# Seven block products in place of eight in the output and gate projections of a decoder layer

## The chip, the cores and the metric

One Trainium2 chip, one core. Times are device microseconds (us). The kernel before takes 2246.29 us, the median of three timed runs (2245.44 to 2246.73).

## The reference

One decoder layer with 1024 tokens and width 2048. Four token mixers (A to D) work on 512 channels each; the two matrices that the change touches, `w_out` and `w_pg`, come behind them.

```python
h = x @ w_in[i]                        # 15 blocks of 512 columns
...                                    # four mixers: y_a, y_b, y_c, y_d
y = jnp.concatenate([y_a * silu(g_a), y_b * silu(g_b),
                     y_c * silu(g_c), y_d * silu(g_d)], axis=-1) @ w_out[i]
x = _layer_norm(ALPHA * x + y, ln_g[i], ln_b[i])
x = x + (p[i] @ w_pe[i]) * jax.nn.sigmoid(x @ w_pg[i])
```

`w_out` and `w_pg` are 2048 x 2048, `w_pe` is 256 x 2048. All is float32.

## The kernel before

**Numbers.** A product of float32 matrices is made of three matmuls: each operand is split into a high part, rounded by a cast on ScalarE (ACT, L142), and a low part, the rest, by a subtraction on VectorE (DVE, L143). TensorE (PE) multiplies high by high, low by high and high by low into the same PSUM bank. A *split* below is this cast and subtraction together.

**First part, to about 1483 us.** The products with `w_in` (proj L188, proj_tok L213) run on PE, and the four mixers are written as Python generators in a queue: step() advances the mixer at its head after every few matmuls, so that its instructions stand between those of the projections. Each mixer ends by storing its 128 channels x 1024 tokens to DRAM as y_dram; the last store is L303, of y_dram3.

**Output projection, L680 to L714.** The mixed channels are loaded back (L636) and split once, into yh and yl. phase2 runs for each half of the tokens (h, 512 tokens) and each of four blocks of 512 columns (n). token_mm (L641, matmul at L650) goes through 16 blocks of 128 channels: for each it loads 128 x 512 of W (load_w, L145 to L152, a DMA of 256 KB), splits it, and does 12 matmuls: four token tiles of 128 by three, into four PSUM banks called tk. So one half and one column block are 192 matmuls, and one projection is 8 x 192 = 1536. DVE then adds the banks to z, which holds x (L690, scaled by ALPHA), and takes the statistics for the layer norm (L691). Weights come twice, once for each token half. The norm of a half (L703, L704 on DVE, with the rows lg and lbias) and the transposes for the next stage (L708) stand in the queue and run beside the next half's matmuls; the normed tokens are stored as xln_dram.

**Gate projection, L716 to L736.** phase3 has the same loops with `w_pg`. Behind each 192 matmuls stand 24 small ones with p and w_pe (L665), ACT's sigmoid, DVE's product and sum (L733, L734, with xr, a piece of xln_dram loaded back), and the store of the result.

**What sets the order.** A tile scheduler orders the instructions by the order in which they are written, and puts what is written under `high_priority(offset=4000)` as far ahead as its buffers allow. Each engine then runs its own instructions in that order; an instruction that waits holds up all behind it on its engine. All DMAs are issued by SyncE (SP), in SP's order. load_w is under high priority, with 3 raw buffers and 4 each of wh and wl. PSUM has two pools of four banks of 512 columns: pp and mx; successive blocks of 192 matmuls take them in turn, so the reads of one set of banks lie beside the matmuls of the other. The pool act has 16 tiles of 1 MB.

Of the kernel before, what the change touches and what calls it, by code (L numbers as in the profile page):

```python
# [41 lines left out]
def trunk_kernel(  # L42
# [44 lines left out]
    # the first loads are under way: load the activation tables, bring the tensor engine up  # L87
# [7 lines left out]
    # softmax over the depth axis, its running sum less the first layer's share  # L95
# [31 lines left out]
    # mixers are traced in steps, a step after every few products of the projections that  # L127
    # follow, so that what a step's products wait for is done when the tensor engine gets there
# [25 lines left out]
    KORD = list(range(4, NK)) + [0, 1, 2, 3]  # L154

    # ======== phase 1: projections and token mixers, channels on partitions ========
    with tc.tile_pool(name="work", bufs=1) as work:
# [41 lines left out]
        def proj_tok(blk, banks, evac_tok, before=lambda k: None):  # L199
            # tokens on partitions: one tile of 128 tokens by 512 channels in each bank  # L200
# [52 lines left out]
        def transpose_to(dst, src):  # L253
            # dst[:, c, :] is the transpose of src[:, c, :], in blocks of 128
# [11 lines left out]
        def rms(o):  # L266
            # o: [token, chunk, channel]; the root mean square is over the head's channels
# [68 lines left out]
        def mix_b(j, kt, lt, qt, gts):  # L336
# [55 lines left out]
            # decays to the chunk's end and from its start  # L392
# [13 lines left out]
            for b in range(2):  # L406
# [3 lines left out]
                # one bank: only its first product clears the marks of what was written  # L410
# [217 lines left out]
        # the mixed channels come back, split, into the slots that x leaves  # L628
        yh = [[act.tile([P, 4, H], F32R, tag="act", name=f"yh{g}{h}") for g in range(4)] for h in range(2)]
        yl = [[act.tile([P, 4, H], F32R, tag="act", name=f"yl{g}{h}") for g in range(4)] for h in range(2)]  # L630
        raws = {}
        free_tags = ("x1", "v1", "E", "W", "a1", "q1", "E", "W", "vt")
        for ki, k in enumerate(KORD):
            tag = free_tags[ki % len(free_tags)]
            raws[k] = wtE() if tag == "E" else wtW() if tag == "W" else wt(tag)
# [170 lines left out]
```

## Time and profile before

| | |
|---|---|
| median of three runs | 2246.29 us |
| span of the profiled execution | 2243.6 us (the profile gives no other time for it) |
| TensorE (PE) busy | 2236.3 us, 100% |
| VectorE (DVE) busy | 958.6 us, 43% |
| ScalarE (ACT) busy | 674.9 us, 30% |
| the output and gate stages | 1483 to 2243.6 us |

Busy shares are of the span. The chain of waits follows the work that ended last back to the start, and its shares say whose time the span is. A grouped line gives the busy time of all its instructions and the mean of one in ns, then the idle time just before them with what ended it.

### The profile page before, as it was taken

To read this page: it belongs to the slowest core of one execution; us is meant where nothing else is said; L and a number is where in the kernel's file an instruction comes from. 1 tells how busy PE (TensorE), PEld (TensorE's weight loads), DVE (VectorE), ACT (ScalarE), POOL (GpSimd) and SP (SyncE) were. 2 spreads that over 40 slices of the span, in tenths; PEclk is the share of its full clock that TensorE was granted. 3 is DMA by queue.
4 is the path that set the end of the run, shared out by engine and by line. 5 is a ranking of instruction groups with operands and counts; after the bars stand their busy time and mean duration, and the time that the engine had idled before them with its cause. 6 is when DMAs were issued, how large, how long until landed. Compare 5 with 4: busy or idle time off the path is not lost.

```text
span 2243.6 us, 26997 instructions
## 1 busy us (share of the span) xinstructions
PE 2236.3 (100%) x10670; PEld 1867.0 (83%) x10670; DVE 958.6 (43%) x1670; ACT 674.9 (30%) x1201; POOL 43.7 (2%) x33
## 2 busy tenths in 40 slices
PE   9999999999999999999999999999999999999999
PEld 8888888888888888888888888888888888888887
DVE  5155565542555755431212212253365358333333
ACT  4144444432432433311211111142223224222222
POOL 0000000000000000000000000000000000000000
PEclk9999999999999999999999999999999999999999
DMA  6311111133111112421211111164345326444443
GB/s 232 96 42 48 46 53 45 56 108 103 43 57 38 57 57 80 142 70 57 94 57 57 50 59 57 48 225 134 96 135 179 113 95 237 133 136 132 136 148 106
DMA packets 112845, 216.33 MB, mean 96 GB/s; under 512 B 11856, under 2 KB 20304, under 8 KB 111440
## 3 DMA queue, kind: packets, MB, share of 16 engines
q1 hardware_dynamic: 112720, 214.62, 30.2%
q8 instruction: 83, 1.36, 0.2%
q14 instruction: 42, 0.34, 0.0%
HBM read 185.22 MB, written 29.36 MB: 96 GB/s over the span
## 4 chain that ended last, share of the span: by engine, by line
PE 99%; DVE 1%; ACT 0%; issue 0%; ACTq 0%; DVEq 0%
PE pp L188 46%; PE tk L650 31%; PE tok L213 12%; PE tk L665 2%; PE gram L362 2%; PE pv L539 1%; PE sc L494 1%; PE att L529 1%; PE sc L495 1%; PE xt L708 1%; PE hgo L414 0%; PE sv L601 0%; PE yt L282 0%; PE gram L347 0%; PE upd L409 0%; PE hgo L431 0%
## 5 line engine op out<-in xcount | busy, mean ns | idle before, releaser
L188 PE MATMUL pp<-xh,wh 128*128 128x512 f32 x1536 | 481.8, 394 | 0.0
L188 PE MATMUL pp<-xl,wh 128*128 128x512 f32 x1536 | 474.5, 390 | 0.0
L188 PE MATMUL pp<-xh,wl 128*128 128x512 f32 x1536 | 473.3, 389 | 0.0
L143 DVE TENSOR_TENSOR wl_t<-raw_t,wh_t 128x512 fp32r<-128x512 f32 x336 | 231.1, 690 | 493.0 <-ACT wh_t L142 452.9
L142 ACT CAST wh_t<-raw_t 128x512 fp32r<-128x512 f32 x336 | 209.2, 623 | 626.4 <-PE tk L650 463.1
L143 DVE TENSOR_TENSOR wl<-raw,wh 128x512 fp32r<-128x512 f32 x192 | 132.5, 690 | 498.0 <-ACT wh L142 483.9
L188 PEld LDWEIGHTS pp<-xl,wh 128*128 128x128 f32 x1536 | 288.4, 188 | 60.8
L188 PEld LDWEIGHTS pp<-xh,wl 128*128 128x128 f32 x1536 | 288.3, 188 | 60.3
L188 PEld LDWEIGHTS pp<-xh,wh 128*128 128x128 f32 x1536 | 281.8, 188 | 53.0
L142 ACT CAST wh<-raw 128x512 fp32r<-128x512 f32 x192 | 119.3, 621 | 637.7 <-PE pp L188 602.7
L650 PE MATMUL tk<-wh_t,yh 128*128 128x512 f32 x512 | 200.8, 392 | 0.0
L650 PE MATMUL tk<-wh_t,th 128*128 128x512 f32 x512 | 200.5, 392 | 0.0
L650 PE MATMUL tk<-wl_t,th 128*128 128x512 f32 x512 | 199.5, 390 | 0.0
L650 PE MATMUL tk<-wh_t,yl 128*128 128x512 f32 x512 | 199.4, 389 | 0.0
L650 PE MATMUL tk<-wl_t,yh 128*128 128x512 f32 x512 | 199.4, 390 | 0.0
L650 PE MATMUL tk<-wh_t,tl 128*128 128x512 f32 x512 | 199.3, 389 | 0.0
L213 PE MATMUL tok<-wh_t,xh 128*128 128x512 f32 x384 | 151.4, 394 | 0.0
L213 PE MATMUL tok<-wh_t,xl 128*128 128x512 f32 x384 | 149.9, 390 | 0.0
L213 PE MATMUL tok<-wl_t,xh 128*128 128x512 f32 x384 | 149.6, 390 | 0.0
L650 PEld LDWEIGHTS tk<-wh_t,yh 128*128 128x128 f32 x512 | 96.1, 188 | 20.2 <-DVE z L690 0.3
L650 PEld LDWEIGHTS tk<-wl_t,th 128*128 128x128 f32 x512 | 96.1, 188 | 20.3
L650 PEld LDWEIGHTS tk<-wl_t,yh 128*128 128x128 f32 x512 | 96.1, 188 | 20.1
(223 smaller groups left out, 2122.5 us busy)
## 6 DMA issues: line engine op xcount, KB each, us to landing
raw<-in_w_in_dram SPq DMA_DIRECT2D x192, 256.0 KB, 2.6
raw_t<-in_w_out_dram SPq DMA_DIRECT2D x128, 256.0 KB, 2.6
raw_t<-in_w_pg_dram SPq DMA_DIRECT2D x128, 256.0 KB, 2.7
raw_t<-in_w_tok_dram SPq DMA_DIRECT2D x80, 256.0 KB, 2.6
z<-in_x_dram SPq DMA_DIRECT2D x32, 256.0 KB, 4.5
xln_dram<-z SPq DMA_DIRECT2D x8, 1024.0 KB, 5.6
xr<-xln_dram SPq DMA_DIRECT2D x32, 256.0 KB, 3.8
out_dram<-sg SPq DMA_DIRECT2D x32, 256.0 KB, 3.1
```

The costliest lines, as they stand in the source:

```text
L142: S.copy(hi, raw)
L143: V.tensor_tensor(lo, raw, hi.bitcast(F32), op=ALU.subtract)
L188: T.matmul(ps[h], lhsT=w[:, c], rhs=xs[q][h][:, kk, :], start=(q == 0 and kk == 0 and w is wh and xs is xh), stop=(q == 3 and kk == 3 and ...
L213: T.matmul(ps[i], lhsT=xs[k // 4][hh][:, k % 4, t], rhs=w, start=(k == 0 and i3 == 0), stop=(k == NK - 1 and i3 == 2),)
L362: T.matmul(psg[:, c, :], lhsT=ls[:, cc], rhs=rs[:, cc], start=True, stop=True)
L494: T.matmul(psc[:, : b - a], lhsT=lhs, rhs=kh[mp][:, a:b], start=True, stop=False)
L495: T.matmul(psc[:, : b - a], lhsT=lhs, rhs=kl[mp][:, a:b], start=False, stop=True)
L529: T.transpose(pst[:, c, :], ch(a_t)[:, 4 * b + c, :], ident)
L539: T.matmul(pso, lhsT=at[:, kb, :], rhs=vtok[:, kb, :], start=(kb == 0), stop=(kb == i))
L650: T.matmul(ps[m], lhsT=a(k)[:, t], rhs=w, start=(ki == 0 and i3 == 0), stop=(ki == len(kord) - 1 and i3 == 2),)
L665: T.matmul(ps[m], lhsT=a(k)[:, t], rhs=ws[k][w], start=(k == 0 and i3 == 0), stop=(k == 1 and i3 == 2),)
L708: T.transpose(ps[:, c, :], t[:, c * P : (c + 1) * P], ident)
```

## The change

Both projections are now computed as seven block products in place of eight. The tokens, the 2048 channels that are summed over and the 2048 columns are each halved. With A11, A12, A21, A22 the blocks of the left matrix (first index: token half; second: channel half) and B11 to B22 those of W, the products are, in the order in which the output projection makes them:

| product | left operand | right operand | goes to |
|---|---|---|---|
| A11 | A11 | b11 | banks psa, then into z: tokens 1, columns 1 |
| S2 | A21 - A22 - A11 | t2 = b11 + b12 + b22 | added onto psa; z: tokens 1, columns 2 |
| S3 | A11 - A21 | t3 = b12 + b22 | onto psa; z: tokens 2, columns 2 |
| A22 | A22 | t4 = b21 + t2 | onto psa; z: tokens 2, columns 1 |
| N1 | A21 - A22 | t1 = b11 + b12 | banks psb; onto z: tokens 2, columns 2 |
| N4 | N1's + A12 - A11 | b22 | onto psb; z: tokens 1, columns 2 |
| A12 | A12 | b21 | onto z: tokens 1, columns 1, one column block at a time |

The signs of what is read from the banks are set where z takes them. Each product is 8 steps of 128 channels: a block of W of 128 x 1024 (512 KB) loaded to a *raw* tile (the pool has five slots), split for two column blocks (th, tl), a block of A split anew each time (ah, al, two buffers each), and 2 x 12 matmuls, into eight banks tk00 to tk13. A product with `cont=True` goes on in the same banks, after DVE has read them.

The sums of W's blocks are made by DVE beside the products (sums23, sum4, sum1), stored to DRAM and loaded back when their product comes. The gate's sums are made during the output projection's A22 and N1 (ops3.sums). The mixed channels stay in float32 (y), and z has eight tiles, loaded by eight DMAs of 1 MB.

In the gate, the products come as N1, A22, A11, S2, S3, A12, N4; N1, A22, A12 and N4 run one column block at a time and load W's blocks of 128 x 1024 again for each. The norm of the second token half stands beside the output projection's N4, its transposes (`turn`) beside A12, and the norm of the first half beside the gate's N1. `ends` is the last stage: the small products with p, whose weights now take three raw tiles for each column block and token half, the product with the sigmoid, the sum with xr, and the store.

```diff
-        raws = {}
...
+        ys = {}
+        for g in YORD:
             for h in range(2):
-                split(hs(raws[k], h), yh[h][k // 4][:, k % 4, :], yl[h][k // 4][:, k % 4, :])
-    # ======== phases 2 and 3: tokens on partitions ========
-    with tc.tile_pool(name="tail", bufs=6, reuse_waits="tile") as tail:
-        big = lambda name, dt=F32: tail.tile([P, 4, H], dt, tag="big", name=name)
-        def token_mm(ps, hi, lo, w_src, kord):
-            for ki, k in enumerate(kord):
-                wh, wl = load_w(w_src[k], "t")
-                for m in range(4):
-                    t = slice(m * P, (m + 1) * P)
-                    for i3, (a, w) in enumerate(((hi, wh), (lo, wh), (hi, wl))):
-                        T.matmul(
-                            ps[m],
-                            lhsT=a(k)[:, t],
-                            rhs=w,
-                            start=(ki == 0 and i3 == 0),
-                            stop=(ki == len(kord) - 1 and i3 == 2),
-                        )
+                ys[g, h] = act.tile([P, 4, H], F32, tag="act", name=f"y{g}{h}")
+                for kk in range(4):
+                    nc.sync.dma_start(ys[g, h][:, kk, :], y_dram[4 * g + kk][:, h * H : (h + 1) * H])
...
+        early = lambda: tc.high_priority(offset=4000)
+        raw_tile = lambda name, dt=F32: tail.tile([P, 2, H], dt, tag="raw", bufs=5, name=name)
...
+            def block(self, r, c, kk):
+                t = raw_tile(f"b{r}{c}")
+                k = self.rows[r - 1][kk]
+                nc.sync.dma_start(t, self.w[2 * c - 2 : 2 * c, k].rearrange("n p w -> p n w"))
+                return t
+            def kept(self, t, kk):
+                s = raw_tile(t)
+                nc.sync.dma_start(s, self.dram[t][kk])
+                return s
...
+            def add(self, out, a, b, name, kk):
+                V.tensor_tensor(out, a, b, op=ALU.add)
+                nc.sync.dma_start(self.dram[name][kk], out)
+            def sums23(self, kk, raw):
+                with early():
+                    b22, b12 = self.block(2, 2, kk), self.block(1, 2, kk)
+                    self.add(b22, b22, b12, "t3", kk)
+                    self.add(b12, b22, raw, "t2", kk)
+            def sum4(self, kk, raw):
+                with early():
+                    b21 = self.block(2, 1, kk)
+                    self.add(b21, b21, raw, "t4", kk)
+            def sum1(self, kk):
+                with early():
+                    b11, b12 = self.block(1, 1, kk), self.block(1, 2, kk)
+                    self.add(b11, b11, b12, "t1", kk)
+            def sums(self, kk):
+                with early():
+                    b11, b12, b22, b21 = (self.block(r, c, kk) for r, c in ((1, 1), (1, 2), (2, 2), (2, 1)))
+                    self.add(b22, b22, b12, "t3", kk)
+                    self.add(b12, b12, b11, "t1", kk)
+                    self.add(b11, b22, b11, "t2", kk)
+                    self.add(b21, b11, b21, "t4", kk)
...
+                    if what == "S3":
+                        V.tensor_tensor(src, a["11"], a["21"], op=ALU.subtract)
+                    else:
+                        V.tensor_tensor(src, a["21"], a["22"], op=ALU.subtract)
+                    if what in ("S2", "N4"):
+                        V.tensor_tensor(src, src, a["11"], op=ALU.subtract)
+                    if what == "N4":
+                        V.tensor_tensor(src, src, a["12"], op=ALU.add)
...
+            def a_split(self, what, kk):
+                hi = tail.tile([P, H], F32R, tag="ah", bufs=2, name="ah")
+                lo = tail.tile([P, H], F32R, tag="al", bufs=2, name="al")
+                split(self.a_comb(what, kk), hi, lo)
+                return hi, lo
+            def b_split(self, raw, n):
+                hi = wpool.tile([P, H], F32R, tag="wh", name="th")
+                lo = wpool.tile([P, H], F32R, tag="wl", name="tl")
+                split(raw[:, n, :], hi, lo)
+                return hi, lo
+        def product(ops, a, b, ps, ns=(0, 1), more=lambda kk, raw: None, cont=False, a_kept=None):
+            for kk in range(8):
+                with early():
+                    raw = ops.b(b, kk)
+                    ws = [ops.b_split(raw, n) for n in ns]
+                    ah, al = ops.a_split(a, kk) if a_kept is None else a_kept(kk)
...
+                                skip_group_check=True,
...
+                more(kk, raw)
                 step()
...
+        def into_z(m, n, ps, op, done):
+            V.scalar_tensor_tensor(z[m][:, n, :], z[m][:, n, :], ALPHA, ps, op0=ALU.mult, op1=op)
...
+        def onto_z(m, n, ps):
+            V.tensor_tensor(z[m][:, n, :], z[m][:, n, :], ps, op=ALU.add)
...
+        for m in range(8):
+            z_in(m)
+        psa = [banks(0), banks(1)]
+        product(ops2, "A11", "b11", psa, more=ops2.sums23)
+        for n, m in pairs:
+            into_z(m, n, psa[n][m], ALU.add, False)
+        product(ops2, "S2", "t2", psa, cont=True, more=ops2.sum4)
+        for n, m in pairs:
+            into_z(m, n + 2, psa[n][m], ALU.subtract, False)
+        product(ops2, "S3", "t3", psa, cont=True, more=lambda kk, raw: ops2.sum1(kk))
+        for n, m in pairs:
+            into_z(4 + m, n + 2, psa[n][m], ALU.subtract, False)
+        product(ops2, "A22", "t4", psa, cont=True, more=lambda kk, raw: kk % 2 or ops3.sums(kk // 2))
...
+        product(ops2, "N1", "t1", psb, more=lambda kk, raw: kk % 2 or ops3.sums(4 + kk // 2))
+        for n, m in pairs:
+            onto_z(4 + m, n + 2, psb[n][m])
...
+        queue.append(norm(1))
+        product(ops2, "N4", "b22", psb, cont=True)
+        for n, m in pairs:
+            onto_z(m, n + 2, psb[n][m])
+        drain()
+        queue.append(turn(1, 0))
...
+            product(ops2, "A12", "b21", psc, ns=(n,))
+            for m in range(4):
+                onto_z(m, n, psc[n][m])
...
+        queue.append(norm(0))
...
+            product(ops3, "N1", "t1", psc, ns=(n,))
...
+                S.copy(p5[n][:, m, :], psc[n][m])
+            if n == 0:
+                drain()
+                queue.append(turn(0, 0))
...
+            product(ops3, "A22", "t4", psc, ns=(n,))
...
+        product(ops3, "A11", "b11", psa)
...
+        product(ops3, "S2", "t2", psa, cont=True)
...
+        product(ops3, "S3", "t3", psa, cont=True)
...
+        def ends(n, sg, half):
+            wr, wh, wl = raw_tile("pe"), raw_tile("peh", F32R), raw_tile("pel", F32R)
+            nc.sync.dma_start(wr, w_pe[n].rearrange("k p w -> p k w"))
+            split(wr, wh, wl)
...
+            product(ops3, "A12", "b21", psc, ns=(n,))
+            one(psc[n], p1, n)
+            queue.append(ends(n, p1[n], 0))
...
+            product(ops3, "N4", "b22", psc, ns=(n,), a_kept=n4_of)
+            one(psc[n], v12, n)
+            queue.append(ends(n + 2, v12[n], 0))
```

How the instructions move, at the three places of which the prediction speaks. A row is line, operation and tile names, with a number for each tile; L664 loads a block of W, L669 loads back a sum, L678 and L679 make and store one, L143 is a split's subtraction, L714 and L716 make a sum of A blocks, L782 reads a bank into z.

The border between the mixers and the output projection, on SP. Before, loads of the first blocks of `w_out` stand ahead of the last loads of y:

```order
L148 DMA raw_35_3_10865<-in_w_in_dram 128x512
L148 DMA raw_t_11035<-in_w_out_dram 128x512
L148 DMA raw_t_11053<-in_w_out_dram 128x512
L148 DMA raw_t_11071<-in_w_out_dram 128x512
L148 DMA raw_t_11089<-in_w_out_dram 128x512
L636 DMA x1_10969<-y_dram13_88 128x1024
L636 DMA v1_10975<-y_dram14_89 128x1024
L636 DMA E_10981<-y_dram15_90 128x1024
L148 DMA raw_t_11107<-in_w_out_dram 128x512
```

The same place after. The last mixer's store (L303) comes first:

```order
L634 DMA y31_10924<-y_dram15_90 128x512
L303 DMA y_dram3_78<-o_10644 128x1024
L634 DMA y00_10929<-y_dram0_75 128x512
L634 DMA y00_10929<-y_dram1_76 128x512
L634 DMA y00_10929<-y_dram2_77 128x512
L664 DMA b11_11039<-in_w_out_dram 128x2x512
L664 DMA b22_11077<-in_w_out_dram 128x2x512
L664 DMA b12_11079<-in_w_out_dram 128x2x512
L664 DMA b11_11085<-in_w_out_dram 128x2x512
```

No block of `w_out` is issued any more before the store of y_dram3.

The first read of banks into z, on DVE. Before, the reads stand between single splits of W:

```order
L143 TENSOR_TENSOR wl_t_11360<-raw_t_11357,wh_t_11359 128x512
L143 TENSOR_TENSOR wl_t_11378<-raw_t_11375,wh_t_11377 128x512
L690 SCALAR_TENSOR_TENSOR z00_11019<-z00_11019,tk0_11031 128x512
L690 SCALAR_TENSOR_TENSOR z01_11020<-z01_11020,tk1_11032 128x512
L691 BN_STATS stats_11023<-z00_11019 128x6
L691 BN_STATS stats_11024<-z01_11020 128x6
L143 TENSOR_TENSOR wl_t_11396<-raw_t_11393,wh_t_11395 128x512
```

After, five sums t4 (b21 + t2) stand ahead of the first read:

```order
L143 TENSOR_TENSOR tl_11463<-t2_11460,th_11462 128x512
L143 TENSOR_TENSOR tl_11467<-t2_11460,th_11466 128x512
L678 TENSOR_TENSOR b21_11501<-b21_11501,t2_11460 128x1024
L678 TENSOR_TENSOR b21_11546<-b21_11546,t2_11505 128x1024
L678 TENSOR_TENSOR b21_11591<-b21_11591,t2_11550 128x1024
L678 TENSOR_TENSOR b21_11636<-b21_11636,t2_11595 128x1024
L714 TENSOR_TENSOR at_11607<-y11_10914,y01_10934 128x512
L716 TENSOR_TENSOR at_11607<-at_11607,y10_10909 128x512
L678 TENSOR_TENSOR b21_11681<-b21_11681,t2_11640 128x1024
L782 SCALAR_TENSOR_TENSOR z0_11015<-z0_11015,tk00_11031 128x512
L782 SCALAR_TENSOR_TENSOR z0_11015<-z0_11015,tk10_11035 128x512
```

And on SP the loads of z (L777), which have no place ahead of the sums now:

```order
L679 DMA ot4_4_10971<-b21_11636 128x1024
L669 DMA t2_11640<-ot2_5_10956 128x1024
L634 DMA y01_10934<-y_dram1_76 128x512
L664 DMA b21_11681<-in_w_out_dram 128x2x512
L634 DMA y01_10934<-y_dram2_77 128x512
L634 DMA y01_10934<-y_dram3_78 128x512
L777 DMA z0_11015<-in_x_dram 128x2048
L679 DMA ot4_5_10972<-b21_11681 128x1024
L777 DMA z1_11017<-in_x_dram 128x2048
L669 DMA t2_11685<-ot2_6_10957 128x1024
L777 DMA z2_11019<-in_x_dram 128x2048
L777 DMA z3_11021<-in_x_dram 128x2048
```

z0 comes behind the store of the sum t4 of step 4 (ot4_4), z2 and z3 behind the load of t2 of step 6.

The product A22, on DVE, where before there were only splits of W one behind the other:

```order
L678 TENSOR_TENSOR b12_12199<-b12_12199,b11_12197 128x1024
L143 TENSOR_TENSOR al_12262<-y31_10924,ah_12261 128x512
L678 TENSOR_TENSOR b11_12197<-b22_12201,b11_12197 128x1024
L143 TENSOR_TENSOR tl_12216<-t4_12213,th_12215 128x512
L143 TENSOR_TENSOR tl_12220<-t4_12213,th_12219 128x512
L678 TENSOR_TENSOR b21_12203<-b11_12197,b21_12203 128x1024
L143 TENSOR_TENSOR al_12316<-y31_10924,ah_12315 128x512
L143 TENSOR_TENSOR tl_12254<-t4_12251,th_12253 128x512
L143 TENSOR_TENSOR tl_12258<-t4_12251,th_12257 128x512
L678 TENSOR_TENSOR b22_12293<-b22_12293,b12_12291 128x1024
```

al_12262 is the low part of A for step 2, tl_12216 and tl_12220 those of W for step 1; al_12316 belongs to step 3, and tl_12254 and tl_12258 to step 2. So a step's A stands one place ahead of the W of the step before it, with the gate's sums (L678) in between.

## Rows read from the trace of the kernel before

**Rows 1.** The page: busy time by engine, and the chain's shares by engine.
```profile
PE 2236.3 (100%) x10670; PEld 1867.0 (83%) x10670; DVE 958.6 (43%) x1670; ACT 674.9 (30%) x1201; POOL 43.7 (2%) x33
...
PE 99%; DVE 1%; ACT 0%; issue 0%; ACTq 0%; DVEq 0%
```

**Rows 2.** Stretches: us, PE, PEld, DVE, ACT, POOL, PE clock, DMA share, GB/s.
```profile
1483.00:1841.00 358.00, 358.00 (x1609) 295.63 (x1608) 161.60 (x256) 94.36 (x155) 4.38 (x4) 1.00 0.44 138
1841.00:2243.60 402.60, 397.97 (x1787) 329.04 (x1785) 173.84 (x269) 117.15 (x193) 4.25 (x4) 1.00 0.46 145
```

**Rows 3.** The chain in order of time: start, us, engine, tile, line, instructions.
```profile
1483.35 181.83 PE tk L650 x802
...
1945.21 43.52 PE tk L650 x192
```

**Rows 4.** Grouped lines of DVE and ACT: busy us, mean ns, idle before.
```profile
L143 DVE TENSOR_TENSOR wl_t<-raw_t,wh_t 128x512 fp32r<-128x512 f32 x336 | 231.1, 690 | 493.0 <-ACT wh_t L142 452.9 <-PE tk L650 26.4 <-PE xt L708 6.1
L142 ACT CAST wh_t<-raw_t 128x512 fp32r<-128x512 f32 x336 | 209.2, 623 | 626.4 <-PE tk L650 463.1 <-PE tok L213 129.4 <-PE tk L665 24.3
...
L704 DVE SCALAR_TENSOR_TENSOR z<-z,lnr,lbias 128x512 f32<-128x512 f32 x32 | 23.1, 745 | 0.0
L703 DVE SCALAR_TENSOR_TENSOR z<-z,lnmv,lg 128x512 f32<-128x512 f32 x32 | 23.0, 746 | 0.0
L734 DVE TENSOR_TENSOR sg<-sg,xr 128x512 f32<-128x512 f32 x32 | 22.2, 692 | 1.1
...
L691 DVE BATCH_NORM_STATS2 stats<-z 128x6 f32<-128x512 f32 x32 | 21.2, 684 | 0.0
L690 DVE SCALAR_TENSOR_TENSOR z<-z,tk 128x512 f32<-128x512 f32 x32 | 20.6, 680 | 0.2 <-DMA z<-in_x_dram 0.2
...
L398 DVE TENSOR_TENSOR q<-q,l 128x1024 f32<-128x1024 f32 x4 | 4.9, 1218 | 0.0
```

**Rows 5.** Timeline at the border: start, us, engine, line, instruction, tiles.
```profile
1483.19 0.39 PE L650 MATMUL tk<-wh_t,yh 128*128 128x512 f32 x1
...
1483.75 1.08 ACT L246 ACTIVATE g<-pp 128x512 f32<-128x512 f32 x2
...
1484.86 1.23 DVE L302 TENSOR_TENSOR o<-o,g 128x1024 f32<-128x1024 f32 x1 [0.21 <-ACT g L246]
...
1486.12 0.33 SPq L303 DMA_DIRECT2D y_dram<-o  x1
```

**Rows 6.** Timeline of SP's queue at the start.
```profile
1.18 0.42 SPq L148 DMA_DIRECT2D raw_t<-in_w_tok_dram  x1
1.65 0.42 SPq L174 DMA_DIRECT2D l<-in_xT_dram  x1
```

**Rows 7.** Stretches with a full DMA queue.
```profile
8.00:20.00 12.00, 12.00 (x54) 9.95 (x53) 10.86 (x17) 9.31 (x17) 0.00 (x0) 1.00 1.03 399
...
1500.00:1520.00 20.00, 20.00 (x90) 16.56 (x89) 5.54 (x8) 4.52 (x8) 0.00 (x0) 1.00 0.87 301
```

**Rows 8.** DMA issues of the whole run: KB each, us to landing.
```profile
raw_t<-in_w_out_dram SPq DMA_DIRECT2D x128, 256.0 KB, 2.6
...
xln_dram<-z SPq DMA_DIRECT2D x8, 1024.0 KB, 5.6
...
y_dram<-o SPq DMA_DIRECT2D x12, 512.0 KB, 2.7
...
v<-in_xT_dram SPq DMA_DIRECT2D x4, 512.0 KB, 5.6
...
W<-y_dram SPq DMA_DIRECT2D x3, 512.0 KB, 4.8
...
lg<-in_ln_rows_dram SPq DMA_DIRECT2D x1, 1024.0 KB, 4.7
lbias<-in_ln_rows_dram SPq DMA_DIRECT2D x1, 1024.0 KB, 7.0
```

**Rows 9.** The first 4 us as a stretch.
```profile
0.00:4.00 4.00, 2.98 (x29) 2.98 (x30) 0.15 (x2) 1.55 (x3) 0.20 (x4) 1.00 0.50 146
```

More of the change, by code (lines that the diff above doesn't have):

```diff
@@ L152, in load_w @@
         return hi, lo
-    KORD = list(range(4, NK)) + [0, 1, 2, 3]
+    YORD = (2, 1, 3, 0)
     with tc.tile_pool(name="work", bufs=1) as work:
@@ L747, in trunk_kernel @@
-        for i in range(4):
-            split(praw[:, i, :], ph[:, i, :], pl[:, i, :])
-        phase3(0, *t0, ph, pl)
-        phase3(1, *t1, ph, pl)
+                    mv, rstd = mvs[m]
+                    t = z[4 * h + m][:, n, :]
+                    V.scalar_tensor_tensor(t, t, mv[:, 0:1], lg[:, n, :], op0=ALU.subtract, op1=ALU.mult)
+                    V.scalar_tensor_tensor(t, t, rstd[:, 1:2], lbias[:, n, :], op0=ALU.mult, op1=ALU.add)
+                    if m % 2 == 1:
+                        yield
@@ new lines, in trunk_kernel @@
+        queue.append(norm(0))
+        p5 = held("p5")
+        for n in range(2):
+            psc = [None, None]
+            psc[n] = banks(0)
+            product(ops3, "N1", "t1", psc, ns=(n,))
+            for m in range(4):
+                S.copy(p5[n][:, m, :], psc[n][m])
+            if n == 0:
+                drain()
+                queue.append(turn(0, 0))
+        p4 = held("p4")
+        for n in range(2):
+            psc = [None, None]
+            psc[n] = banks(0)
+            product(ops3, "A22", "t4", psc, ns=(n,))
+            for m in range(4):
+                S.copy(p4[n][:, m, :], psc[n][m])
@@ new lines, in one @@
+        def one(psn, q, n):
+            for m in range(4):
+                V.tensor_tensor(q[n][:, m, :], q[n][:, m, :], psn[m], op=ALU.add)
+                S.activation(q[n][:, m, :], q[n][:, m, :], AF.Sigmoid)
+        for n in range(2):
+            queue.append(ends(n + 2, p5[n], 1))
+        for n in range(2):
+            queue.append(ends(n, p4[n], 1))
+        for n in range(2):
+            psc = [None, None]
+            psc[n] = banks(0)
+            product(ops3, "A12", "b21", psc, ns=(n,))
+            one(psc[n], p1, n)
+            queue.append(ends(n, p1[n], 0))
@@ new lines, in trunk_kernel, with n4_of @@
+        n4 = [None] * 4
+        def n4_of(kk):
+            g, q = kk // 4, kk % 4
+            if q == 0 and n4[2 * g] is None:
+                for i in range(2):
+                    n4[2 * g + i] = act.tile([P, 4, H], F32R, tag="act", name=f"n4{g}{i}")
+            pair = n4[2 * g][:, q, :], n4[2 * g + 1][:, q, :]
+            if (g, q) not in n4_done:
+                n4_done.add((g, q))
+                split(ops3.a_comb("N4", kk), *pair)
+            return pair
+        n4_done = set()
@@ L753, in _layout @@
+        for n in range(2):
+            psc = [None, None]
+            psc[n] = banks(0)
+            product(ops3, "N4", "b22", psc, ns=(n,), a_kept=n4_of)
+            one(psc[n], v12, n)
+            queue.append(ends(n + 2, v12[n], 0))
+        drain()
 def _layout(inputs):
```

209 lines of the change are left out of this document (124 added, 85 removed).

## The prediction

> **What bounds the kernel now.** I read the busy shares and the chain of waits first: TensorE (PE) is busy 100% of the span and makes 99% of the chain [rows 1]. The table by stretches says the same of the two output stages: from 1483 to 2243.6 us PE has hardly a gap, while VectorE (DVE) works 161.6 + 173.8 = 335 of 761 us and the DMA engines 45% [rows 2]. So time is PE's, and it is counted in matmuls: the chain in order of time has a run of 192 matmuls of the gate in 43.52 us, 226.7 ns each [rows 3]. The grouped lines then give what each DVE and ACT operation costs [rows 4], the timeline the border between the mixers and the output projection [rows 5, 6], and the stretches and the DMA list what the queue can move [rows 7, 8]. The profile has a span (2243.6 us) and no time of its own; the median of the timed runs lies 2.7 us above it, and I add that at the end.
>
> **What goes.** Each projection had 8 x 16 x 4 x 3 = 1536 matmuls and gets 7 x 192 = 1344. Both together lose 384 x 0.2267 = **87.0 us** of PE's row. The transposes and the 192 small products with p stay. If all that is added stays hidden, 87 us is the gain.
>
> **What is added, as loads on the cover.** DVE in the tail: 368 splits and 120 sums of A blocks at 0.69, 64 sums of W blocks at 1.22, 56 + 32 for z and its statistics at 0.68, 64 for the norm at 0.745, 40 + 64 for the gate's ends at 0.69, 10 splits of 1024 columns at 1.22 [rows 4]: 606 us, where PE will have 761 - 87 = 674. DVE was a bystander with 335 and is now level with PE; where stages differ, it is the later one. The queue: a block of W is 0.524 MB. The first five products (A11, S2, S3, A22, N1 of the output projection) load and store 40 + 24 + 32 + 40 + 40 = 176 such blocks, as the sums of the gate's weights are made there too, and with z, the late part of y, lg and lbias it is 104.9 MB against 217.6 us of matmuls. The best the queue does in the trace over 12 us is 399 GB/s, and 301 is what it does in a stretch of loads in the order of the work [rows 7]: 263 to 348 us. So in these five products transfers alone cost 45 to 131 us more than PE.
> The Trainium skill (DMA: Bandwidth & Descriptors, Specifications) puts a core's share of HBM at about 358 GB/s, by which the same bytes would take 293 us, an estimate; this trace went above it, 399 over 12 us, on one core, so I do not use it as a ceiling.
>
> Now by place, with the order in which each engine's instructions stand.
>
> **1. The border.** Before, weights for the output projection were loaded ahead of the last store of y. Now the first b11 stands in SP behind that store, which waits for DVE's product. That chain exists in the trace: the next stage's first matmul at 1483.2, two activations, the product, the store at 1486.1 [rows 5], so 2.9 us. Four more issues at 0.47 [rows 6] make 4.8. A 512 KB transfer lands after 2.7 us when little is queued and 5.6 when much is [rows 8]; the store and three loads are ahead, I take 4.5. Then a cast and most of a subtraction, 0.9 [rows 4]. PE idles **10** us where it idled none (8.4 to 11.3).
>
> **2. The first product, A11.** Each of its 8 steps (5.44 us of PE) loads b11, b22, b12 and stores t3, t2. In SP the load of the next b12 stands behind the store of t2; in DVE the next t3 needs that b12, then stands a split of A, then t2, then its store. The loop is issue 0.5 + landing + 1.22 + 0.69 + 1.22: with 4.5 for the landing 8.1 us a step. Its bytes at 399 GB/s take 6.6. Six of the eight steps pay 2.7: **16** us (at landings of 2.7 and 5.6: 5 and 23).
>
> **3. z.** S2 adds onto the banks of A11, so its matmuls wait until DVE has read them into z, and z must have landed. In SP z0 stands behind t4 stores, and in DVE the reads stand behind the sums t4_1 to t4_5, of which the first comes after a split that waits for PE to leave A11's last step. From PE's end of A11: 0.62 + 0.69 + 2 x 1.22 to the sum t4_2 (3.8); its store lands (3.4), b21_4 lands (3.4), sum (12), store t4_4 lands (15.4), b21_5 and z0 are issued (17), b21_5 lands, two subtractions, sum t4_5 (21.5), its store lands (25), t2_6, z2 and z3 are issued (26), 1 MB lands after 4.7 to 7.0 (32.5), two reads, PE's last 12 matmuls (37). Meanwhile PE does 48 matmuls, 10.9 us, as each z comes. Lost: **26** us. I took 3.4 for a landing, near the 2.7 of the quiet store; five such lie in the chain, so 20 with 2.7 and the shorter z, 33 with 4.8 [rows 8].
>
> **4. S2 and S3.** A split after that wait 2; the reads between S2 and S3 stand among splits, 2; S3 moves 4 blocks a step and lg, lbias: 18.9 MB, 47 us at 399 against 43.5, some fetched in S2. Together **10** (4 to 22, the latter at 301 GB/s).
>
> **5. A22 and N1.** In DVE the split of A for step k+2, which waits for PE to finish step k, stands ahead of W's split for step k+1. After PE's end of a step DVE still has cast wait 0.62, 0.69, up to two sums of 1.22, an A sum of 0.69 and the split 0.69: 2.0, 3.2, or 4.5 to 5.2 us, less 2 to 5 matmuls that PE has ahead. Over A22 that is 15 us, over N1 12; at N1's start PE has 40 matmuls (9.1 us) while DVE has 14.5 us until the last bank is read, 5 more. The bytes ask 52.6 us of each at 399, 9 over PE, and 70 at 301. I take 18 and 20: **38** (20 to 60).
>
> **6. N4 and the first A12.** The norm of the second half runs on DVE here. N4: 48 splits and sums 33.1, 16 reads and statistics 10.9, 32 of the norm 23.8: 68 us beside 43.5. The splits come in time; the excess of 24 falls before the first read that A12 waits for, and some of it is hidden behind splits made ahead. **20** (8 to 28).
>
> **7. The gate's first product, with the norm of the first half:** 32 splits, 16 sums, 8 reads, 32 of the norm: 65 us of DVE beside 43.5; the gate's A22 after it has room. **13** (5 to 22).
>
> **8. The rest of the gate.** The ends take three of the five raw slots, so at each of eight changes of column block the next W load waits (10); N4's first half has DVE 5.0 us a step beside 4.1 of PE (7); the end has the reads behind the last product (1). **18** (4 to 30).
>
> Sum of the waits: 10 + 16 + 26 + 10 + 38 + 20 + 13 + 18 = 151. Less 87.0: **+64**. 2243.6 + 64 + 2.7 = **2310 us**. All lower ends together give -13, all upper ends +142; they will not fall together, half the distance gives this case 2270 to 2350.
>
> **Rivals.**
> *A, the queue keeps up (faster).* Its place is the loop of store, load and sum in places 2 to 5. If loads run so far ahead that only bytes count, places 1 to 5 cost 263 - 218 = 45 instead of 100, and places 6 to 8 their lower ends, 17. Net -25: 2221. It decides when the waits sum to less than 87. For it: 399 GB/s over 12 us [rows 7], and DVE idles 56% of the tail before [rows 2]. Against it: five raw slots cannot run ahead of a step that uses three to five, and z's chain is latency, not bytes.
> *B, the queue does 301 GB/s.* Places 1 to 5 cost 348 - 218 = 130, the rest 51: +94, 2340. For it: that stretch of the trace had loads placed among waits as here, half loads, half stores is not in the trace at all. Against: there SP had little to issue.
> *C, all is hidden.* 2246 - 87 = 2159. For it: the shares of rows 2. Against: 104.9 MB in 218 us would be 482 GB/s, over anything in rows 7.
> The clock is none of the sums: the granted clock is 1.00 in the first 4 us and everywhere after [rows 9, 2], so no row has a price for it. The Trainium skill (TensorE: Matmul & The Clock Gate, Part 1) says the array falls to half clock after idling and returns when busy; by that rule waits as long as in places 1, 3 and 6 would each cost some us more, which no run here shows yet.
>
> **How the numbers follow.** Forecast 0.50; B and worse 0.22; A 0.18; C 0.03; the gap between A and the forecast 0.07, of which 0.04 within 0.2% (4.5 us, about what a measurement can tell from no change) and 0.03 just slower. So faster 0.21, same 0.04, slower 0.75. The range takes B's centre and more, and A's centre: 2215 to 2365.
>
> **What would show it.** Place 1: the first A11 matmul some 10 us after the last of the mixers. 2: A11's runs of 24 matmuls every 8 us instead of 5.4, DVE waiting for b12. 3: PE waiting for the read of z, longest single wait, over 20 us, with z0 landing after A11's end. 4, 5: DMA near full share in S3, A22, N1, and PE waiting for W's lower parts; these two products over 60 us each. 6, 7: DVE without idle time while PE waits for z's reads and splits. 8: PE waits at each W_pe load. I am wrong if the five products take under 265 us, or if PE's waits in the tail sum to under 87 us; and wrong on the other side if A11 to N1 take over 350.

## The result: slower by 3%, and the profile after

The changed kernel takes 2313.38 us (median of four runs, 2312.18 to 2316.15) where the one before takes 2246.51 in the same runs: a ratio of 1.0299 (95% interval 1.0285 to 1.0314), or 67 us more. The forecast was 2310.

The page of the changed kernel, busy time and the chain's shares, beside [rows 1]:

```profile
PE 2189.9 (95%) x10286; PEld 1808.6 (78%) x10286; DVE 1167.8 (51%) x1956; ACT 720.9 (31%) x1295; POOL 44.6 (2%) x33
...
PE 87%; DMA 7%; DVE 4%; ACT 1%; issue 1%; SPq 0%; DVEq 0%; ACTq 0%
```

PE has 384 matmuls fewer and is no longer the whole chain. Its busy time fell by 46.4 us, though 384 matmuls at 226.7 ns [rows 3] are 87: most of the rest is matmuls that ran at the lower clock (in A11 below, 53.3 us busy for 192 matmuls, which are 43.5 at the full one). The table by stretches of the changed kernel, one line for each stage from the border on, beside [rows 2] (us, PE, PEld, DVE, ACT, POOL, PE clock, DMA share, GB/s):

```profile
1483.40:1494.60 11.20, 0.00 (x0) 0.00 (x0) 6.24 (x10) 2.57 (x6) 0.00 (x0) 0.71 0.98 322
1494.60:1559.20 64.60, 53.30 (x192) 40.71 (x192) 33.59 (x40) 12.60 (x22) 0.00 (x0) 0.87 0.88 308
1559.20:1597.40 38.20, 0.04 (x2) 0.06 (x1) 13.84 (x16) 2.79 (x5) 0.00 (x0) 0.55 0.88 310
1597.40:1645.30 47.90, 46.28 (x195) 37.50 (x196) 30.33 (x46) 13.31 (x23) 0.00 (x0) 0.97 0.90 329
1645.30:1689.40 44.10, 44.07 (x194) 35.62 (x192) 31.29 (x45) 13.20 (x24) 0.00 (x0) 1.00 0.95 332
1689.40:1754.70 65.30, 50.49 (x194) 38.21 (x193) 41.65 (x53) 13.83 (x25) 0.00 (x0) 0.92 0.89 320
1754.70:1821.50 66.80, 51.98 (x194) 39.25 (x193) 52.45 (x70) 14.10 (x25) 0.00 (x0) 0.90 0.89 324
1821.50:1876.10 54.60, 45.68 (x193) 36.05 (x192) 54.31 (x94) 15.31 (x27) 3.21 (x4) 0.95 0.49 160
1876.10:1929.50 53.40, 53.40 (x257) 43.41 (x255) 36.40 (x60) 25.65 (x48) 0.00 (x0) 0.96 0.59 198
1929.50:1978.00 48.50, 47.90 (x225) 39.03 (x225) 48.41 (x85) 25.61 (x48) 6.33 (x4) 1.00 0.53 172
1978.00:2156.00 178.00, 178.00 (x801) 147.19 (x800) 98.23 (x150) 78.12 (x137) 0.00 (x0) 1.00 0.44 147
2156.00:2227.00 71.00, 66.31 (x290) 53.51 (x288) 54.64 (x85) 31.63 (x53) 0.00 (x0) 1.00 0.71 223
2227.00:2311.00 84.00, 71.77 (x286) 55.71 (x285) 59.13 (x90) 23.19 (x36) 0.00 (x0) 0.94 0.68 216
```

The lines are: border, A11, the wait for z, S2, S3, A22, N1, N4, A12; then the gate's N1, the run of A22, A11, S2 and S3, then A12 and N4 with the ends. Two things are to be seen. From the border to the end of N1 the DMA engines are 0.88 to 0.98 busy in every line and move 308 to 332 GB/s. And in the output projection the granted clock is below 1.00 in the lines in which PE waits; in the gate's A12 it stays at 1.00 although PE waits 4.8 us there in all. 2.4 GHz is the full level, and a mean of 0.92 or 0.87 is a mixture with the half one. The bounds of the lines are read to about half a microsecond, the end of N4 to 1.4.

What each place cost is its duration less 0.2267 us for each matmul (43.5 for 192; A12 and the gate's N1 also less 0.48 for each set of transposes, 16 and 8: 12 matmuls and a set take 3.21 us there, 1955.10 to 1958.31 in the chain in order of time, and 12 matmuls alone 2.72):

| place | predicted | measured |
|---|---|---|
| 1 border | 10 | 11.2 |
| 2 A11 | 16 | 21.1 |
| 3 wait for z, and S2 behind it | 26 | 38.2 + 4.4 |
| 4 S2, S3 | 10 | 0.6 (S3; S2 is counted in 3) |
| 5 A22 and N1 | 38 | 21.8 + 23.3 |
| 6 N4 and A12 | 20 | 13.3 |
| 7 gate's N1 | 13 | 1.2 |
| 8 rest of the gate | 18 | 19.3 (what is left) |
| sum | 151 | 154.4 (2311.0 - 2243.6 + 87.0) |

PE's waits in the changed kernel from the border to the end of N1 (us in total, times, longest):

```profile
PE tk L744 <- ACT th L142: 44.1, 17, 11.2
PE tk L744 <- DVE z L782: 41.1, 4, 38.2
PE tk L744 <- DVE tl L143: 6.7, 7, 2.1
```

The longest is the read of A11's banks into z. The chain of waits shows how it came about (start, us, what):

```profile
1572.57 1.24 DVE b L678
...
1573.83 3.90 DMA ot<-b
...
1577.78 4.46 DMA b<-in_w_out_dram
...
1582.33 1.24 DVE b L678
...
1583.58 4.32 DMA ot<-b
...
1587.91 4.45 DMA b<-in_w_out_dram
...
1592.48 1.24 DVE b L678
...
1593.74 4.00 DMA ot<-b
...
1598.17 7.34 DMA z<-in_x_dram
```

It is the chain that the prediction wrote down for place 3, turn by turn: sum t4, its store, the next load of b21, the next sum, and z's loads behind the stores. (z0, whose read ended the wait of 38.2 us, was issued at 1589.38 and landed at 1596.51; the last line is z2, for which PE waited 1.6 us more.) By this view alone the case looks settled, with the order in SP as its cause. The experiments say otherwise.

### The profile page after: what moved, and what is told of

The parts are those of the page before. It is cut to its first block, busy times and chain, and to the rows that moved or that the text cites. A ratio compares the mean times of both kernels' runs of the same rounds, so it can differ in the third digit from the quotient of the medians.

```text
span 2311.0 us, 26611 instructions
## 1 busy us (share of the span) xinstructions
PE 2189.9 (95%) x10286; PEld 1808.6 (78%) x10286; DVE 1167.8 (51%) x1956; ACT 720.9 (31%) x1295; POOL 44.6 (2%) x33
## 4 chain that ended last, share of the span: by engine, by line
PE 87%; DMA 7%; DVE 4%; ACT 1%; issue 1%; SPq 0%; DVEq 0%; ACTq 0%
PE pp L188 45%; PE tk L744 22%; PE tok L213 11%; DMA b<-in_w_out_dram 2%; DMA b<-in_w_pg_dram 2%; PE gram L362 2%; PE pv L539 1%; DMA t<-ot 1%; DVE b L678 1%; DMA ot<-b 1%; PE pse L919 1%; PE sc L494 1%; PE att L529 1%; PE sc L495 1%; DVE tl L143 1%
## 5 line engine op out<-in xcount | busy, mean ns | idle before, releaser
L744 PE MATMUL tk<-th,ah 128*128 128x512 f32 x832 | 337.8, 408 | 99.4 <-ACT th L142 48.8
L143 DVE TENSOR_TENSOR wl<-raw,wh 128x512 fp32r<-128x512 f32 x192 | 132.6, 691 | 497.8 <-ACT wh L142 483.7
L744 PE MATMUL tk<-tl,ah 128*128 128x512 f32 x832 | 330.2, 401 | 6.7 <-DVE tl L143 6.7
L744 PE MATMUL tk<-th,al 128*128 128x512 f32 x832 | 332.7, 400 | 0.0
L744 PEld LDWEIGHTS tk<-th,ah 128*128 128x128 f32 x832 | 161.1, 194 | 145.7 <-ACT th L142 57.2
L744 PEld LDWEIGHTS tk<-tl,ah 128*128 128x128 f32 x832 | 160.9, 194 | 46.0 <-DVE tl L143 11.5
L744 PEld LDWEIGHTS tk<-th,al 128*128 128x128 f32 x832 | 161.7, 194 | 33.5 <-DVE al L143 1.8
L142 ACT CAST th<-t 128x512 fp32r<-128x512 f32 x128 | 77.3, 620 | 213.9 <-PE tk L744 160.7
L143 DVE TENSOR_TENSOR tl<-t,th 128x512 fp32r<-128x512 f32 x128 | 86.1, 688 | 69.3 <-ACT th L142 63.4
L143 DVE TENSOR_TENSOR wl_t<-raw_t,wh_t 128x512 fp32r<-128x512 f32 x80 | 55.0, 690 | 111.8 <-ACT wh_t L142 104.3
L143 DVE TENSOR_TENSOR tl<-b,th 128x512 fp32r<-128x512 f32 x96 | 65.2, 689 | 58.3 <-ACT th L142 58.0
```

What stands on the lines that cost most here:

```text
L142: S.copy(hi, raw)
L143: V.tensor_tensor(lo, raw, hi.bitcast(F32), op=ALU.subtract)
L744: T.matmul(ps[n][m], lhsT=l[:, t], rhs=w, start=(not cont and kk == 0 and i3 == 0), stop=(kk == 7 and i3 == 2), skip_group_check=True,)
```

## The experiments

Two accounts were tested. The *chain*: loads stand behind stores that wait for DVE, so latencies add up (the prediction's places 2 to 5). The *bytes*: from the border to the end of N1 the kernel moves 108 MB (320 GB/s by 338.1 us), the DMA engines are full, and a wait that is taken away in one place comes back in another.

**t4_late.** The sums t4 without high priority, so that z's loads and reads stand ahead of them.

```diff
             def sum4(self, kk, raw):
-                with early():
-                    b21 = self.block(2, 1, kk)
-                    self.add(b21, b21, raw, "t4", kk)
+                b21 = self.block(2, 1, kk)
+                self.add(b21, b21, raw, "t4", kk)
```

> The sums t4 of the output projection lose their high priority, so that in DVE and in SP they stand behind the reads of A11's banks, and the loads of z stand ahead of them. Nothing is left out. Bytes and instructions are the same. The account of the prediction (a chain of store, load and sum holds z): PE's wait between A11 and S2, 38 us in the changed kernel, falls to about 12, S2 pays some of it back in waits for t2 (5 to 10), span about 15 to 20 shorter than the changed kernel's 2311. Rival (the queue is full from A11 to N1, 0.87 to 0.95 busy at 304 to 332 GB/s, so only bytes count): what is saved before S2 comes back in S2, S3 and A22, span within 5 us of 2311.

Measured 2305.69 us, ratio 1.0264 (1.0249 to 1.0279), 7.7 under the changed kernel (the profiled spans differ by 4.8). The wait for z fell from 38.2 to 12.8 us, as the chain has it, but S2 then waited 10.9 for the weights of its second step, and N4 began at 1820.3 where it had begun at 1820.8. Of 25 us saved about half a microsecond was left there; what was gained came behind it, in N4, 4 us shorter. This is nearer to the forecast by bytes (within 5) than to that by the chain (15 to 20).

**pool_store.** The 64 stores issued by POOL.

```diff
                 V.tensor_tensor(out, a, b, op=ALU.add)
-                nc.sync.dma_start(self.dram[name][kk], out)
+                nc.gpsimd.dma_start(self.dram[name][kk], out)
```

> The changed kernel with the 64 stores of sums issued by POOL, whose queue is empty, in place of SP. Nothing is left out and the bytes are the same; loads no longer stand behind a store that waits for DVE, and the loads of z now stand among A11's. If the order in SP's queue is what costs (the prediction's chain of store, load and sum): the wait for z (38 us) goes, A11 loses half of its 21 over PE, and A22 and N1 some: 2313 - 45 or more, under 2270. If the DMA engines' bandwidth is what costs (105 MB between the border and the end of N1 at 314 to 330 GB/s): A11 to N1 still end about 320 to 330 us after the border, waits only change places, 2300 to 2315. I expect the latter in the main, with some gain where the queue stood still: 2295.

Measured 2321.86, ratio 1.0335 (1.0321 to 1.0349): slower than the changed kernel by 8.5. The wait for the reads of A11's banks was gone, and A11, S2 and S3 became longer, 81.5, 57.2 and 62.6 us: 201 together, where they had taken 195 with the wait for z. The gain that I had expected with the free queue did not come. The stores now took longer to land, 7.3 us for those of the output projection's sums and 4.6 for the gate's (medians), where the changed kernel has 3.1 and 2.9; whether that is why N4 began 3.6 us later was not tested.

**fill.** Small matmuls with a zero operand in PE's gaps, to hold the clock up.

```diff
+                if ops.name == "o" and a in ("A11", "A22", "N1") and kk >= 1:
+                    for _ in range(20):
+                        T.matmul(ps[0][0][:, 0:P], lhsT=idle, rhs=idle, start=False, stop=False, ...)
```

> In A11, A22 and N1 of the output projection 20 matmuls of 128 columns with a zero operand (about 1.1 us of PE) go onto an open bank ahead of each step but the first, 23 times: 26 us of PE's work, most of it in gaps where PE waits in the changed kernel. The sums are unchanged. The changed kernel's matmuls after such gaps run at the lower of the two granted clocks, and these three products hold 26 us beyond their waits. If that lower clock is on the path: 10 to 18 us shorter than the changed kernel, 2295 to 2303, with the granted clock of these stretches up from 0.89 to 0.92 towards 1.00. Rival (the queue sets these products' time, so a faster PE only waits longer): within 5 us of 2313. If the filling itself is in the way: 10 us or more longer.

(The edit puts them in 21 times, 420 matmuls, and not 23 times.) Measured 2311.00, ratio 1.0287 (1.0272 to 1.0303): no clear difference from the changed kernel's 1.0299, as the rival had it. The stretches of A22 and N1 of the changed kernel, in this one:

```profile
1689.00:1755.00 66.00, 58.24 (x359) 45.41 (x358) 42.40 (x56) 13.57 (x24) 0.00 (x0) 0.99 0.89 320
1755.00:1822.00 67.00, 55.82 (x309) 42.85 (x308) 51.88 (x70) 15.02 (x26) 0.00 (x0) 0.94 0.87 316
```

The clock went from 0.92 and 0.90 to 0.99 and 0.94, and the products took 64.6 and 67.8 us in place of 65.3 and 66.8, with PE still waiting. So the slow matmuls there filled time in which PE would have waited. A11 alone gained 5 us, and of these 2 were left where N4 begins.

**gate_no_store** and **gate_no_add.** Of the gate's sums in A22 and N1 either the stores or the additions are left out.

```diff
...
                 V.tensor_tensor(out, a, b, op=ALU.add)
-                nc.sync.dma_start(self.dram[name][kk], out)
+                if self.name == "o":
+                    nc.sync.dma_start(self.dram[name][kk], out)
```
```diff
-                V.tensor_tensor(out, a, b, op=ALU.add)
+                if self.name == "o":
+                    V.tensor_tensor(out, a, b, op=ALU.add)
                 nc.sync.dma_start(self.dram[name][kk], out)
```

> The sums of the gate's weights are loaded and added as in the changed kernel, but their 32 stores of 512 KB are left out, and the gate loads blocks of w_pg in place of the sums (the same number and size), so its values are not the layer's. DVE's instructions and their order stay. By the queue: A22 and N1 together move 25 MB in place of 42, 78 us at 321 GB/s, under PE's 87: their 45 us over PE fall to 5 to 15, span 30 to 40 shorter, 2271 to 2281. By DVE's order (the split of A ahead of W's, with sums between): they keep 25 us or more of the 45, span at most 20 shorter.

> The 32 additions for the gate's sums in A22 and N1 are left out, and the loaded blocks are stored as they are, so the gate's values are not the layer's; loads and stores and their bytes stay. DVE loses 39 us of 95 in these two products. If the queue alone holds them: 132 us together as in the changed kernel, at most 8 less, span 2303 to 2313. If DVE's order does: 110 or less, span under 2293. With the stores left out they took 110, so both have a part, and I expect about 120, span 2300.

Measured 2293.96, ratio 1.0206 (1.0189 to 1.0223), without the stores, and 2307.71, ratio 1.0274 (1.0257 to 1.0291), without the additions. The two products without the stores, A22 and then N1:

```profile
1690.90:1742.00 51.10, 46.22 (x192) 35.45 (x193) 39.96 (x50) 14.32 (x25) 0.00 (x0) 1.00 0.78 269
1742.00:1801.00 59.00, 49.28 (x194) 37.83 (x193) 52.25 (x72) 14.64 (x26) 0.00 (x0) 0.91 0.71 236
```

and the same two without the additions, in the stretches of the changed kernel:

```profile
1689.00:1755.00 66.00, 52.85 (x215) 40.31 (x214) 29.76 (x49) 14.26 (x26) 0.00 (x0) 0.97 0.98 358
1755.00:1822.00 67.00, 51.42 (x187) 36.81 (x186) 32.97 (x53) 14.47 (x27) 0.00 (x0) 0.92 0.86 304
```

A third of DVE's work less changed them from 132.1 us to 128.9; 17 MB less, with all of DVE's work in its order, to 110.1. That it is the stores' bytes, and not their place in SP's queue, is seen beside pool_store, which took the same stores out of that queue and kept the bytes: 128.8 us. So the queue holds these two products first. What holds the 23 us that are left over PE's 87 is not shown: the DMA engines are at 0.78 and 0.71 and DVE at 0.78 and 0.89, which speaks for DVE, but no run left out both the stores and the additions. My two forecasts do not meet: without the stores the span fell by 19, as DVE's order had it (at most 20, against 30 to 40 by the queue), and without the additions by 6, as the queue alone had it (at most 8, against the 13 that I expected). Each limit seems to cover the other.

**no_gate_sums.** All that belongs to the gate's sums left out of A22 and N1.

```diff
...
-        product(ops2, "A22", "t4", psa, cont=True, more=lambda kk, raw: kk % 2 or ops3.sums(kk // 2))
+        product(ops2, "A22", "t4", psa, cont=True)
...
-        product(ops2, "N1", "t1", psb, more=lambda kk, raw: kk % 2 or ops3.sums(4 + kk // 2))
+        product(ops2, "N1", "t1", psb)
```

> Leaves out the sums of the gate's weights (their 32 loads, 32 sums and 32 stores of 512 KB) that stood beside the output projection's A22 and N1; the gate loads blocks of w_pg in their place, so its own loads stay the same in number and size, and the gate's values are not the layer's. Both accounts: A22 and N1, 65.3 and 66.8 us in the changed kernel, go to 44 to 48 each, since their transfers fall to two blocks a step or fewer; span 36 to 44 us shorter, about 2271. If they stay over 55 each, it is the order of A's and W's splits in DVE and not what the sums bring.

Measured 2268.74, ratio 1.0100 (1.0085 to 1.0115), 44.6 less:

```profile
1688.60:1732.20 43.60, 43.60 (x194) 35.89 (x193) 22.59 (x37) 14.49 (x26) 0.00 (x0) 1.00 0.43 143
1732.20:1776.80 44.60, 44.29 (x194) 35.75 (x193) 34.39 (x55) 14.18 (x25) 0.00 (x0) 1.00 0.30 95
```

A22 and N1 are at PE's pace. The order of the splits of A and W in DVE, which place 5 charged first, costs nothing when the sums are away.

**sums_early.** The same 64 sums, made during the last projections of `w_in`.

```diff
+        def presums():
+            for i in range(16):
...
+                four = [wt(t) for t in ("x1", "v1", "a1", "q1")] if i % 2 == 0 else [wtE(), wtE(), wtW(), wtW()]
...
+        queue.append(presums())
         for j in range(4):
             unit_a(j)
+        drain()
...
-        product(ops2, "A11", "b11", psa, more=ops2.sums23)
+        product(ops2, "A11", "b11", psa)
```

(The other products lose their sums likewise.)

> All 64 sums of W's blocks are made and stored during the last projections of w_in, where in the kernel before DVE is busy a fifth of the time and the DMA engines too, in tiles that stand idle there; nothing is left out. A11 to N1 then load one block a step and store none. If the sums' loads, adds and stores are what A11 to N1 wait for (by chain or by bytes): A11 loses its 21 us over PE, the wait for z falls from 38 to under 6, A22 and N1 lose 35 to 45; the border's 11, N4, A12 and the ends stay. Span 2311 - 100 = about 2210 (2195 to 2225), faster than the kernel before. Rival: the sums' 78 us of DVE and 67 MB in the earlier stretch hold up the mixers or the loads of w_in, and PE waits there 20 us or more: 2230 or worse.

Measured 2205.68, ratio 0.9818 (0.9804 to 0.9833): 107.7 under the changed kernel and 41 under the one before. The stretch before the border, in the kernel before and in this one, and A11 to N1 in this one:

```profile
1130.00:1483.00 353.00, 353.00 (x1559) 292.37 (x1559) 86.65 (x121) 61.91 (x106) 0.00 (x0) 1.00 0.20 64
1130.00:1483.00 353.00, 352.85 (x1557) 291.95 (x1555) 103.27 (x122) 47.66 (x79) 0.00 (x0) 1.00 0.44 148
1494.00:1715.00 221.00, 220.67 (x960) 181.45 (x961) 129.54 (x202) 71.08 (x122) 0.00 (x0) 0.99 0.46 158
```

The sums cost PE nothing that can be seen where they now stand, and the five products take 221 us against 217.6 for their matmuls. After A11's first matmul no single wait of PE in them is above 0.4 us. This run takes away the chain and the bytes together, so it shows that the sums beside these products cost the time, and not by which of the two.

**early_br** and **early_pe.** On top of the early sums: the first W of A11 through the small tiles and the reads of N4's banks ahead of the norm; or the ends' raw weights in the small tiles.

```diff
+                    if ops.name == "o" and a == "A11" and kk == 0:
+                        raw = None
+                        ws = [load_w(w_out[n, YROWS[0]], "t") for n in ns]
...
         product(ops2, "N4", "b22", psb, cont=True)
-        for n, m in pairs:
-            onto_z(m, n + 2, psb[n][m])
+        with early():
+            for n, m in pairs:
+                onto_z(m, n + 2, psb[n][m])
```
```diff
-            wr, wh, wl = raw_tile("pe"), raw_tile("peh", F32R), raw_tile("pel", F32R)
...
+            wh, wl = raw_tile("peh", F32R), raw_tile("pel", F32R)
+            for k in range(2):
+                wr = wpool.tile([P, H], F32, tag="raw", bufs=3, name="pe")
```

> The version with early sums, and two edits: the first block of W of A11 comes through the small weight tiles, loaded ahead of the last store of y; and the reads of N4's banks into z have high priority, ahead of 16 instructions of the norm in DVE. Nothing is left out. Border: 11 us of idle PE fall to about 7, since A's first low part still waits in DVE for that store (it landed at 1488.0 in the run with early sums). A12's first wait, 7.0 us, falls under 1. Sum: 2205.7 - 4 - 6 = about 2196. Rival: the norm, put later, makes the transposes late, and what A12 gains comes back in the gate's first product: 2202.

> The version with early sums, and in the gate's ends the raw weights of p's product go to the small weight tiles that are idle there, so that an end takes two of the five raw slots and not three. Nothing is left out. If the slots hold up the loads of w_pg (the prediction's place 8): PE's waits in A12 and N4 of the gate, 11 us in the run with early sums, fall by 4 to 8, 2198 to 2202. Rival (DVE, 0.72 to 0.77 busy there, and its order): within 2 us of 2205.7.

Measured 2192.72, ratio 0.9760 (0.9746 to 0.9775), and 2201.56, ratio 0.9800 (0.9785 to 0.9814). In the first A11 ended 4.3 us sooner: its first matmuls, in the timeline of PE, now stop for the low part of A, which stands in DVE behind a sum of A blocks (L734) that waits for the last store of y:

```profile
1484.19 0.96 PE L768 MATMUL tk<-wh_t,ah 128*128 128x512 f32 x3 [1.45 <-ACT ah L142]
1488.22 1.29 DVE L734 TENSOR_TENSOR at<-y,y 128x512 f32<-128x512 f32 x2 [3.33 <-DMA y_dram<-o]
1490.17 0.79 PE L768 MATMUL tk<-wh_t,al 128*128 128x512 f32 x1 [5.01 <-DVE al L143]
```

A12's first wait of 7.0 us is gone, and what follows it did not become later: 8 us there, 1 of them since A12's first half then ran at a granted clock of 1.00 in place of 0.94. In the second the gate from A12 to the end took 150.1 us in place of 155.0: the slots are a part of place 8 in that version.

**best.** The edits of the last two together.

> Early sums, the first block of W ahead of the border, the reads of N4's banks ahead of the norm, and the ends' raw weights in the small tiles: the edits of the two runs before taken together, nothing left out. Their places lie apart (border and A12 of the output projection; A12 and N4 of the gate), so the gains add: 2205.7 - 13.0 - 4.1 = 2188.6, that is 57 us under the kernel before. If the ends' gain only moves to the last products' DVE work, 2192.

Measured 2188.51 (five runs), ratio 0.9741 (0.9728 to 0.9754): 58 us under the kernel before, and 29 us of the 87 are still not had, for the most part in the gate's last two products.

## Why the prediction was right, and where its steps were wrong

The time was right (2310 for 2313.38), and so was the balance, 151 of waits against 87. That it was right to 3 us is luck: places 1, 2, 3, 5 and 8 were put too low by 31 us together (place 3 alone by 17), and places 4, 6 and 7 too high by 28. As stated: the border held (10, measured 11.2; the version with W loaded ahead shows the next thing late behind it), A11 and the rest of the gate are within about 5 us, z had the longest wait, with z landing after A11's end, and A22 and N1 were over 60 us each. One sign did not come: there PE was to wait for W's lower parts, which stand behind A's split in DVE. It waited 6.1 us for them and 22.2 for the casts (ACT th), which themselves waited for loads of the sums (DMA t, 34.4 us).

The step that was wrong in kind is how places 2 to 5 were priced. I added latencies of one chain after another, and kept the bytes as rival B, at 301 GB/s. The trace has that chain, but t4_late and pool_store, which undo it in different ways, and fill, which helps PE, gain no more than 2 us up to the start of N4. The stretch from the border to about the start of N4 (its first matmul is at 1820.8, 1820.3, 1818.9 and 1824.5), for the changed kernel, t4_late, fill and pool_store in turn:

```profile
1483.40:1821.50 338.10, 246.17 (x963) 191.35 (x964) 209.38 (x276) 72.39 (x126) 0.00 (x0) 0.87 0.90 320
```
```profile
1483.40:1820.30 336.90, 250.56 (x961) 191.10 (x961) 212.66 (x282) 71.18 (x125) 0.00 (x0) 0.90 0.90 320
```
```profile
1483.40:1819.50 336.10, 261.90 (x1383) 206.85 (x1384) 208.54 (x276) 71.83 (x125) 0.00 (x0) 0.90 0.90 320
```
```profile
1483.40:1826.20 342.80, 263.27 (x964) 200.79 (x965) 206.28 (x274) 72.02 (x128) 34.25 (x64) 0.88 0.90 316
```

The same bytes at 316 to 320 GB/s and a DMA share of 0.90, whatever waits for what. So the border and these five products cost 338.1 - 217.6 = 120.5, mostly by the queue's rate, where the chains gave 100 and rival B 130. But 320 is not the most that the queue does in this mixture: without the additions A22 ran at 358 and a share of 0.98. At that rate 108 MB would take about 302 us (an estimate from these two numbers), so some 36 of the 120 us need not be the queue's, and what keeps its share at 0.90 is open. Rival A's rate, 399, was not kept over any of these stretches. The prediction set aside the Trainium skill's 358 GB/s for a core (DMA: Bandwidth & Descriptors, Specifications) because of the 399 of [rows 7]. Over the long stretches the trace stays under the page's figure, 316 to 320 over 336 to 343 us, and comes up to it in the 66 us without the additions.

Place 4 (10, measured 0.6): 16 of S2's 24 transfers were issued during the wait for z, so the queue had room for S3's; in t4_late, where that wait was 12.8 us, S3 took 48.4. Place 7 (13, measured 1.2): DVE was full there, 48.4 of 48.5 us, but the splits were ahead of the norm in it, and the norm's last instruction came at 1988.8, 11 us into the gate's A22, which had room; no one waited for it. Place 6 was put too high by 7; about 8 of its 13 us are the reads of N4's banks behind the norm, as the run that moved these reads showed in the version with early sums. The price of DVE in both was too high as well. Place 7's 65 us is 62 by its own rows, and a sum of the mean durations of [rows 4] is not the time of the engine where its instructions stand back to back: each of 128 x 512 then lasts 0.69 us, but the next starts 0.60 after it (0.75 and 0.66 in the norm):

```profile
1975.52 0.67 DVE L143 TENSOR_TENSOR al<-xt,ah 128x512 fp32r<-128x512 f32 x1
1976.12 0.67 DVE L716 TENSOR_TENSOR at<-at,xt 128x512 f32<-128x512 f32 x1
```

Over both stages DVE's durations sum to 608.8 us, as forecast (606), but the engine was busy 560.5.

The clock got no price, with no row for it then. It fell in the long waits, to a mean of 0.55 of full in that for z. The Trainium skill (TensorE: Matmul & The Clock Gate, Part 1) says that the array runs at half clock after idling, and the trace agrees where the wait was long: the first matmuls after the 38.2 us start 0.43 us apart in place of 0.23. It did not add to the time in A22 and N1, as fill shows. Where only PE was late, it did. With the sums early, A11 and S2 have 192 matmuls each and no wait after A11's first one, which follows the 11 us of the border (stretches of A11, S2):

```profile
1493.90:1539.83 45.93, 45.93 (x192) 37.77 (x193) 19.99 (x32) 14.64 (x26) 0.00 (x0) 0.95 0.89 333
1539.83:1583.37 43.54, 43.54 (x193) 36.02 (x192) 28.86 (x47) 14.06 (x25) 0.00 (x0) 1.00 0.46 157
```

So a wait of 11 us cost 2.4 us more behind it.

The loss does not lie in the seven products themselves: with their sums elsewhere they are faster than eight.

## What to carry to other kernels

When work is added to a stage, sum its bytes first and divide by a rate that the queue keeps over the whole stage and in the same mixture of loads and stores; if that is over the engine's time, the chain of waits can show where the queue's time surfaces and not what causes it. Work that depends on weights alone belongs in a stretch where DVE and the DMA engines have room, however early. And a version that moves one wait is a cheap test: if the end of the stage stays, as it did in t4_late, the wait was a symptom.

## Not expected

Taking the stores from SP's queue to POOL's made the kernel 8.5 us slower, although loads were free to run ahead. And the 64 sums, with 67 MB of transfers, beside the last projections cost PE 0.15 us of 353, at a DMA share of 0.44 where the kernel before has 0.20.
